# Folding two gain vectors into weight rows, and moving elementwise work off GpSimd, in a one-core decoder layer

## The chip, the cores and the metric

One core of a Trainium2 chip runs the whole program. The metric is device microseconds of one execution, the median over several runs. Engines are named as in the profile: PE is TensorE's matrix multiply (PEld its weight load), DVE is VectorE, ACT is ScalarE, POOL is GpSimd, SP is SyncE, whose queue issues nearly all transfers.

## The reference, cut to what matters

```python
h = rms_norm(x, g_mix)
z = h @ w_in                       # u, gb, gc, q, k, v
y_conv = gb * short_conv(gc * u, conv_w)
y_attn = dilated_mixture(q, k, v)  # q, k normed per head
mix = concat(rms_norm(y_conv, g_conv_out), rms_norm(y_attn, g_attn_out))
x = x + mix @ w_out
h = rms_norm(x, g_ffn)
x = x + (silu(h @ w_gate) * (h @ w_up)) @ w_down
# rms_norm(x, g) = x * rsqrt(mean(x*x) + 1e-6) * g ; SEQ 2048, D 1024, D_FF 2816, float32
```

A gain `g` that multiplies the columns of a normalised activation can as well multiply the rows of the weight that follows: `(n * g) @ W = n @ (diag(g) W)`. That identity is what the change uses, for `g_attn_out` with the lower half of the rows of `w_out`, and for `g_ffn` with the rows of `w_gate` and `w_up`.

## The kernel before, in words

Every float32 operand of a matrix product is held as two float16 parts, high and low, and each product is three passes on PE (high by high, high by low, low by high). Weights are first scaled by a power of two found from their largest absolute value (`vmax`, then `pow2`), then split: ACT writes the high part, DVE the low part as scaled input minus high part.

The stages, in the order of the profile's time:

- Up to about 245 us: the norm of `x`, the first projection with the gated convolution (`conv_steps`), and, in between, the splitting of later weights into DRAM. `spill_pair` does this for `w_out`, two column blocks of 256 at a time: L169 on ACT and L170 on DVE, each over 128 x 2048 elements.
- Up to about 856 us: attention, head pair by head pair (`attn_steps`), with the next pair's projections and the tail of the convolution woven in.
- About 856 to 1065 us, called the output stage here: `out_b`, a loop over p = 0 to 7, each pass with two row tiles of 128 (rows p and p + 8). `prep(p)` loads the attention output, squares it on ACT (L777), multiplies it by the row `g_attn_out` on POOL (L778), scales and splits it (L784 on ACT, L785 on DVE), and transposes it by transfers on SP's queue. `tiles(p)` runs the lower half of the output projection (`out_half`), adds each PSUM bank to the residual on DVE (L803, evacuation), squares the sum on ACT (L808), makes the norm's factor on DVE in a few tiny instructions (`rnorm`, L61 to L66), multiplies by factor and `g_ffn` on DVE (L812), forms four Strassen-Winograd sums on POOL (L816 to L819), and splits seven blocks into `hl` (ACT L825; L826 on DVE, the first of the four on POOL), which SP stores to `d_h` (L827). `out_a(p + 1)` runs the upper half of the projection for a later pass: split of its input (L728 on ACT, L729 on DVE), evacuation (L741 on DVE; L743 on ACT, then L744 on POOL). For p = 3 and 5 the first two calls of `left` are made here.
- From about 1040 to 1860 us: the gate and up products in the seven-product Winograd form, 11 rounds f. `left` prepares each round's weights, once for gate and once for up: load of 128 x 2048 elements into `raw`, `vmax` (L88) and `pow2` on DVE, four sums on POOL (L852 to L855), seven splits (L868 on ACT, L869 on DVE). `down` does the same for `w_down` and stores to DRAM (L908 to L914).
- To the end: the down product (L1069).

The queue of each engine is in order. Their order comes from a planner that simulates the program when it is built; `issue_after(x)` holds the instructions made inside it behind `x` on the engine of `x`. The `left` calls of p = 3 and 5 stand behind `self.dve`, `self.act` and `self.sp`.

Buffers that matter: `raw` (pool `wq`) has two, `t` of the Winograd sums one, `hl` one, the split weights `w` fifteen.

Of the kernel before, what the change touches and what calls it, by code (L numbers as in the profile page):

```python
# [29 lines left out]
class Builder:  # L30
# [22 lines left out]
    def rnorm(self, pool, ss, n, d, tag):  # L53


        nc = self.nc
        e = nc.vector
        y = pool.tile([P, n], F32, name=f"{tag}_y")
        t = pool.tile([P, n], F32, name=f"{tag}_t")
        v = pool.tile([P, n], F32, name=f"{tag}_v")  # L60
        nc.scalar.activation(y, ss, AF.Sqrt, scale=1.0 / d, bias=self.eps)  # L61
        e.tensor_scalar(v, ss, 1.0 / d, EPS, op0=ALU.mult, op1=ALU.add)
        e.reciprocal(y, y)
        e.scalar_tensor_tensor(t, y, -0.5, y, op0=ALU.mult, op1=ALU.mult)
# [91 lines left out]
    def spill_pair(self, cols, ux, dst, un):  # L156

        nc = self.nc
        raws = []
        for ap in cols:  # L160
            raw = self.wraw.tile([P, KC, 256], F32, name="wraw")
            nc.sync.dma_start(raw, ap.rearrange("(c p) n -> p c n", p=P))
            raws.append(raw)
        s, u = self.pow2(self.wsm, self.vmax(*(r.rearrange("p k c -> p (k c)") for r in raws)), "w", 14, 14)
        nc.vector.tensor_tensor(un, u, ux, op=ALU.mult)
        for i, raw in enumerate(raws):
            wh = self.wsp.tile([P, KC, 256], F16, name="wh")
            wl = self.wsp.tile([P, KC, 256], F16, name="wl")
            nc.scalar.activation(wh, raw, AF.Copy, scale=s)  # L169
            nc.vector.scalar_tensor_tensor(wl, raw, s, wh, op0=ALU.mult, op1=ALU.subtract)  # L170
            nc.sync.dma_start(dst[:, 0, :, 256 * i:256 * (i + 1)], wh)
            nc.sync.dma_start(dst[:, 1, :, 256 * i:256 * (i + 1)], wl)
# [21 lines left out]
    def run(self):  # L194
        tc, nc, A = self.tc, self.nc, self.A
        with ExitStack() as ctx:
# [16 lines left out]
            self.eps = cp.tile([P, 1], F32, name="eps")  # L213
# [16 lines left out]
    def setup(self):  # L230

        nc, A, cp = self.nc, self.A, self.cp
        make_identity(nc, self.ident32)
        nc.vector.memset(self.ones, 1.0)
        nc.vector.memset(self.eps, EPS)
# [396 lines left out]
    def attention_pairs(self):  # L632
# [28 lines left out]
        self.g_at_row = self.rows.tile([P, 512], F32, name="g_row3")  # L661
        nc.scalar.dma_start(self.g_at_row, A["g_attn_out"][0].partition_broadcast(P))
        nc.vector.tensor_scalar_mul(self.g_at_row, self.g_at_row, self.g_out[2])
# [84 lines left out]
    def out_b(self):  # L748
        tc, nc, A = self.tc, self.nc, self.A
        with ExitStack() as c:  # L750
            e = c.enter_context
            op = self.op = e(tc.tile_pool(name="op", bufs=1))
            g_at = self.g_at_row
            g_ffn = op.tile([P, D], F32, name="g_row2")
            nc.sync.dma_start(g_ffn, A["g_ffn"][0].partition_broadcast(P))
            self.g_ffn = self.row_scale(g_ffn, "gffn", 7)
            nc.vector.tensor_scalar_mul(g_ffn, g_ffn, self.g_ffn[1])
# [3 lines left out]
            def prep(p):  # L761
# [20 lines left out]
                r = self.rnorm(op, ss, 2, 512, "opr")  # L782
# [7 lines left out]
            def tiles(p, mt):  # L790
# [6 lines left out]
                for j in range(2):  # L797
# [23 lines left out]
                for src, q, n, e_ in ((xs[0].rearrange("p (a b) -> p a b", a=2), 0, 2, nc.gpsimd),  # L821
# [4 lines left out]
                    e_.tensor_tensor(o[:, :, 1], src, o[:, :, 0], op=ALU.subtract)  # L826
# [39 lines left out]
    def wsplit(self, x, s):  # L866
        w = self.fw.tile([P, 2, 4, P], F16, name="w")
        self.nc.scalar.activation(w[:, 0], x, AF.Copy, scale=s)  # L868
        self.nc.vector.scalar_tensor_tensor(w[:, 1], x, s, w[:, 0], op0=ALU.mult, op1=ALU.subtract)  # L869
        return w  # L870

    def left(self, w, f):
# [14 lines left out]
        for n in self.ORDER:  # L887
            W[n] = self.wsplit(src[n], s)
# [258 lines left out]
```

## Time and profile before

| what | value |
|---|---|
| median of 3 runs | 2265.3 us (2264.29 to 2267.96) |
| the profiled execution | 2265.61 us, its span 2263.8 us |
| mean granted TensorE clock | 0.973 |
| PE busy | 2134.7 us (94%) |
| DVE busy | 1538.1 us (68%) |
| ACT busy | 937.2 us (41%) |
| POOL busy | 787.9 us (35%) |
| SP's queue, share of 16 transfer engines | 55.9% |

The span runs from the first to the last instruction; what lies around it is the difference to the execution's time, 1.8 us. Busy shares are means over stages with different limits, so they say where to look and not what a change is worth.

### The profile page before, as it was taken

The page shows a single profiled execution, that of the slowest core. Times are in us where ns is not written, and L with a number is a line of the kernel's source. Part 1 is how long each engine was busy: PE and PEld are TensorE (multiplying, and loading weights), DVE is VectorE, ACT ScalarE, POOL GpSimd, SP SyncE. Part 2 cuts the span into 40 slices and gives each one's busy share as a digit, 9 for nine tenths or more (in the row PEclk, how much of TensorE's full clock was granted, in tenths as well). Part 3 has the DMA queues.
Part 4 walks back from the last instruction along what each step waited for, and adds up shares of the span by engine and source line. Part 5 has one row for each costly group of instructions (what it writes and reads, how often), then busy time and mean ns, then how long its engine had stood idle before and what let it go on. Part 6 is the DMA issues. An engine that isn't in the chain of part 4 may idle for free.

```text
span 2263.8 us, 32997 instructions
## 1 busy us (share of the span) xinstructions
PE 2134.7 (94%) x11816; PEld 1070.1 (47%) x11816; DVE 1538.1 (68%) x3265; ACT 937.2 (41%) x2112; POOL 787.9 (35%) x591
## 2 busy tenths in 40 slices
PE   4898999999999979788999999999999999999999
PEld 2344566666565544333444444444444444444444
DVE  6776457888777678796677676676767565555554
ACT  5422236666566655443333233233322343333341
POOL 3010243445444116554122122122222225555463
PEclk9999999999799989999999999999999999999999
DMA  9776356889789987669933322333223455152342
GB/s 242 163 227 224 95 125 126 185 153 168 170 154 183 215 207 222 217 186 257 222 117 107 98 89 89 103 112 99 88 98 105 144 171 203 56 186 60 118 144 93
DMA packets 568052, 340.68 MB, mean 150 GB/s; under 512 B 370896, under 2 KB 520400, under 8 KB 565456
## 3 DMA queue, kind: packets, MB, share of 16 engines
q1 hardware_dynamic: 564672, 337.72, 55.9%
q8 instruction: 92, 1.51, 0.3%
q10 hardware_dynamic: 3216, 0.86, 0.2%
q14 instruction: 72, 0.59, 0.1%
HBM read 162.34 MB, written 107.48 MB: 119 GB/s over the span
## 4 chain that ended last, share of the span: by engine, by line
PE 43%; DMA 4%; DVE 4%; SPq 3%; issue 1%; ACT 1%; POOL 1%; DVEq 0%; ACTq 0%; POOLq 0%
PE ps L951 25%; PE ps L1069 18%; SPq L191 2%; DMA d_wd<-w 1%; DVE w L869 1%; DMA wq<-in_w_up_dram 1%; DMA wq<-in_w_gate_dram 1%; ACT w L868 1%; DMA wq<-d_a 1%; DVE hl L826 0%; DVE vm_a L88 0%; DVE s L957 0%; DVE b L729 0%; SPq L877 0%; ACT wq L1047 0%
## 5 line engine op out<-in xcount | busy, mean ns | idle before, releaser
L951 PEld LDWEIGHTS <-w 128*128 128x128 f16 x3696 | 363.0, 98 | 459.4 <-issue 22.4
L951 PE MATMUL ps<-b,w 128*128 128x512 f16 x2112 | 469.5, 383 | 15.0 <-DVE s L957 6.7
L1069 PE MATMUL ps<-b,w 128*128 128x512 f16 x1848 | 399.3, 379 | 0.9 <-DVE s L1087 0.8
L951 PE MATMUL ps<-hb,w 128*128 128x512 f16 x1584 | 347.4, 379 | 0.9 <-DVE s L957 0.9
L1069 PEld LDWEIGHTS <-w 128*128 128x128 f16 x1848 | 180.8, 98 | 219.2 <-issue 1.4
L852 POOL TENSOR_TENSOR t<-wq 128x512 f32<-128x512 f32 (+1 forms) x46 | 59.1, 1285 | 501.8 <-issue 226.2
L581 ACT ACTIVATE sm<-sm,u 128x256 f32<-128x256 f32 (+1 forms) x384 | 173.9, 456 | 67.8 <-DVE u L576 65.9
L868 ACT ACTIVATE w<-t,w_s 128x512 f16<-128x512 f32 x132 | 94.8, 720 | 248.7 <-PE ps L951 120.4
L957 DVE TENSOR_TENSOR s<-ps,s 128x512 f32<-128x512 f32 x220 | 149.2, 684 | 41.3 <-PE ps L951 39.6
L576 DVE CUSTOM_DVE_ANT_0 sm<-s,mask,nkap 128x256 f32<-128x256 f32 (+1 forms) x384 | 144.1, 420 | 44.7 <-PE s L572 25.0
L183 PE MATMUL mm<-wq,b 128*128 128x384 f16 x512 | 171.7, 335 | 0.0
L184 PE MATMUL mm<-wq,b 128*128 128x384 f16 x512 | 171.4, 335 | 0.0
L185 PE MATMUL mm<-wq,b 128*128 128x384 f16 x512 | 171.1, 334 | 0.0
L1076 POOL TENSOR_TENSOR x<-x,s 128x512 f32<-128x512 f32 x72 | 103.2, 1434 | 186.0 <-DVE s L1087 131.3
L869 DVE SCALAR_TENSOR_TENSOR w<-t,w_s,w 128x512 f16<-128x512 f32 x132 | 98.8, 749 | 96.0 <-ACT w L868 95.9
L1077 DVE SCALAR_TENSOR_TENSOR x<-ps,a_u,x 128x512 f32<-128x512 f32 x96 | 72.0, 750 | 112.5 <-PE ps L1069 83.9
L868 ACT ACTIVATE w<-wq,w_s 128x512 f16<-128x512 f32 x99 | 71.3, 720 | 180.5 <-PE ps L951 66.9
L572 PE MATMUL s<-kb,qT 128*128 128x256 f16 (+1 forms) x384 | 131.1, 357 | 2.6 <-DMA kb<-klz 2.6
L571 PE MATMUL s<-ka,qT 128*128 128x256 f16 (+1 forms) x384 | 129.9, 355 | 2.9 <-DVE u L576 1.9
L593 DVE TENSOR_TENSOR eh<-sm,eh 128x512 f16<-128x512 f32 (+1 forms) x112 | 101.3, 907 | 40.8 <-ACT eh L592 40.3
L184 PEld LDWEIGHTS <-b 128*128 128x128 f16 x768 | 77.6, 101 | 90.6 <-issue 33.4
L183 PEld LDWEIGHTS <-b 128*128 128x128 f16 x768 | 77.6, 101 | 75.5 <-issue 6.9
(296 smaller groups left out, 3723.4 us busy)
## 6 DMA issues: line engine op xcount, KB each, us to landing
d_a<-a SPq DMA_DIRECT2D x88, 256.0 KB, 2.0
d_wd<-w SPq DMA_DIRECT2D x77, 256.0 KB, 2.0
wq<-d_a SPq DMA_DIRECT2D x64, 256.0 KB, 4.2
b<-d_wd SPq DMA_DIRECT2D x14, 1024.0 KB, 5.7
wraw<-in_w_in_dram SPq DMA_DIRECT2D x24, 512.0 KB, 7.3
v<-d_v SPq DMA_DIRECT2D x24, 512.0 KB, 4.6
d_h<-hl SPq DMA_DIRECT2D x24, 512.0 KB, 3.8
wq<-in_w_gate_dram SPq DMA_DIRECT2D x22, 512.0 KB, 5.2
```

The costliest lines, as they stand in the source:

```text
L183: self.pe = mm(ps, lhsT=lh(k), rhs=rh(k), start=k == ks[0], stop=False)
L184: mm(ps, lhsT=lh(k), rhs=rl(k), start=False, stop=False)
L185: mm(ps, lhsT=ll(k), rhs=rh(k), start=False, stop=k == ks[-1])
L571: nc.tensor.matmul(sp[:, at[u]], lhsT=q, rhs=cols(ka, u, pv), start=True, stop=False)
L572: nc.tensor.matmul(sp[:, at[u]], lhsT=q, rhs=cols(kl, u, pv), start=False, stop=True)
L576: nc.vector.tensor_tensor_reduce(sm[:, at[u]], sp[:, at[u]], self.mask[:, P - P * has_prev(u):256], accum_out=Ub[:, u, HD + 1:HD + 2], op0 ...
L581: nc.scalar.activation(sm[:, at[u]], sm[:, at[u]], AF.Exp, scale=-1.0, bias=Ub[:, u, HD + 1:HD + 2], accum_out=Ub[:, u, HD:HD + 1])
L868: self.nc.scalar.activation(w[:, 0], x, AF.Copy, scale=s)
L869: self.nc.vector.scalar_tensor_tensor(w[:, 1], x, s, w[:, 0], op0=ALU.mult, op1=ALU.subtract)
L951: nc.tensor.matmul(ps[self.BANK[n]], lhsT=w[:, x, k], rhs=b[:, y, k], start=first and k == 0 and q == 0, stop=k == 3 and q == 2, skip_grou ...
L957: nc.vector.tensor_tensor(t, x, y, op=ALU.add)
L1069: nc.tensor.matmul(ps[self.BANK[n]], lhsT=L[n][:, x, f], rhs=B[n][:, f, y], start=first and f == 0 and q == 0, stop=f == n_f - 1 and q == ...
```

## The change

`g_attn_out` no longer multiplies the attention output: `spill_pair` multiplies rows 512 to 1023 of `w_out` by it while it splits them, in five pieces for each column block (one of 128 x 1024, four of 128 x 256, each with its own factor column) instead of one. `g_ffn` no longer multiplies the normed activation: `left` multiplies the eight row blocks of each gate and up weight tile by it, in place, in eight ACT instructions of 128 x 256, ahead of the POOL sums; its seven splits are then without a factor. The two gain rows broadcast over partitions (L662 with L663, L755 with the lines behind it) go away; `g_ffn` is loaded as a 128 x 8 column tile on ACT's queue by `gains`. In the output stage L778 goes away, L812 moves from DVE to ACT, L816 to L819 and the first L826 move from POOL to DVE. `self.act` is now the scaling on ACT, `self.dve` the last L826. Powers of two shift between the factors (`SHIFTS`).

```diff
-    def rnorm(self, pool, ss, n, d, tag):
+    SHIFTS = (0, 8, 9)
+    def rnorm(self, pool, ss, n, d, tag, shift=0):
+        f = 4.0 ** -shift
...
-        nc.scalar.activation(y, ss, AF.Sqrt, scale=1.0 / d, bias=self.eps)
-        e.tensor_scalar(v, ss, 1.0 / d, EPS, op0=ALU.mult, op1=ALU.add)
+        b = self.SHIFTS.index(shift)
+        nc.scalar.activation(y, ss, AF.Sqrt, scale=f / d, bias=self.eps[:, b:b + 1])
+        e.tensor_scalar(v, ss, f / d, f * EPS, op0=ALU.mult, op1=ALU.add)
...
@@ spill_pair
-        s, u = self.pow2(self.wsm, self.vmax(...), "w", 14, 14)
+        s, u = self.pow2(self.wsm, self.vmax(...), "w", 13, 13)
         nc.vector.tensor_tensor(un, u, ux, op=ALU.mult)
+        sg = self.wsm.tile([P, 4], F32, name="w_sg")
+        nc.vector.tensor_scalar(sg, self.g_out[0][:, 4:8], s, 2.0 ** -9, op0=ALU.mult, op1=ALU.mult)
         for i, raw in enumerate(raws):
             wh = self.wsp.tile([P, KC, 256], F16, name="wh")
             wl = self.wsp.tile([P, KC, 256], F16, name="wl")
-            nc.scalar.activation(wh, raw, AF.Copy, scale=s)
-            nc.vector.scalar_tensor_tensor(wl, raw, s, wh, op0=ALU.mult, op1=ALU.subtract)
+            for k, f in [(slice(0, 4), s)] + [(4 + k, sg[:, k:k + 1]) for k in range(4)]:
+                nc.scalar.activation(wh[:, k], raw[:, k], AF.Copy, scale=f)
+                nc.vector.scalar_tensor_tensor(wl[:, k], raw[:, k], f, wh[:, k], op0=ALU.mult, op1=ALU.subtract)
...
@@ attention_pairs
-        self.g_at_row = self.rows.tile([P, 512], F32, name="g_row3")
-        nc.scalar.dma_start(self.g_at_row, A["g_attn_out"][0].partition_broadcast(P))
-        nc.vector.tensor_scalar_mul(self.g_at_row, self.g_at_row, self.g_out[2])
...
@@ out_b
-            g_ffn = op.tile([P, D], F32, name="g_row2")
-            nc.sync.dma_start(g_ffn, A["g_ffn"][0].partition_broadcast(P))
-            self.g_ffn = self.row_scale(g_ffn, "gffn", 7)
-            nc.vector.tensor_scalar_mul(g_ffn, g_ffn, self.g_ffn[1])
+            self.g_ffn = self.gains(self.cp, [A["g_ffn"][0]], "gffn", 0)
+            self.u_ffn = self.cp.tile([P, 1], F32, name="u_ffn")
+            nc.vector.tensor_scalar_mul(self.u_ffn, self.g_ffn[1], 2.0 ** -8)
...
@@ prep
                         nc.scalar.activation(hl[:, j, 0, cs], yb[:, j, cs], AF.Square, accum_out=ss[:, q, j:j + 1])
-                        nc.gpsimd.tensor_tensor(yb[:, j, cs], yb[:, j, cs], g_at[:, cs], op=ALU.mult)
...
@@ tiles
-                    self.act = nc.scalar.activation(xn, x1, AF.Square, accum_out=ss[:, j:j + 1])
+                    nc.scalar.activation(xn, x1, AF.Square, accum_out=ss[:, j:j + 1])
                     xs.append(xn)
-                r = self.rnorm(op, ss, 2, D, "n2")
+                r = self.rnorm(op, ss, 2, D, "n2", 8)
                 for j in range(2):
-                    self.dve = nc.vector.scalar_tensor_tensor(xs[j], self.x1[p][j], r[:, j:j + 1], g_ffn, op0=ALU.mult,
-                                                              op1=ALU.mult)
+                    self.act = nc.scalar.activation(xs[j], self.x1[p][j], AF.Copy, scale=r[:, j:j + 1])
...
-                g = nc.gpsimd
+                g = nc.vector
                 g.tensor_tensor(t[:, 1], b12, b11, op=ALU.subtract)
                 g.tensor_tensor(t[:, 3], b22, b12, op=ALU.subtract)
                 g.tensor_tensor(t[:, 2], b22, t[:, 1], op=ALU.subtract)
                 g.tensor_tensor(t[:, 0], b21, t[:, 2], op=ALU.subtract)
                 hl = op.tile([P, 7, 2, 512], F16, name="hl")
-                for src, q, n, e_ in ((xs[0].rearrange("p (a b) -> p a b", a=2), 0, 2, nc.gpsimd),
+                for src, q, n, e_ in ((xs[0].rearrange("p (a b) -> p a b", a=2), 0, 2, nc.vector),
...
-                    e_.tensor_tensor(o[:, :, 1], src, o[:, :, 0], op=ALU.subtract)
+                    self.dve = e_.tensor_tensor(o[:, :, 1], src, o[:, :, 0], op=ALU.subtract)
...
@@ wsplit, left
+        if s is None:
+            self.nc.scalar.copy(w[:, 0], x)
+            self.nc.vector.tensor_tensor(w[:, 1], x, w[:, 0], op=ALU.subtract)
...
-        nc.vector.tensor_tensor(un, u, self.g_ffn[0], op=ALU.mult)
+        nc.vector.tensor_tensor(un, u, self.u_ffn, op=ALU.mult)
+        sg = self.wsm.tile([P, KC], F32, name="w_sg")
+        nc.vector.tensor_scalar_mul(sg, self.g_ffn[0], s)
+        for k in range(KC):
+            nc.scalar.activation(raw[:, k], raw[:, k], AF.Copy, scale=sg[:, k:k + 1])
...
-            W[n] = self.wsplit(src[n], s)
+            W[n] = self.wsplit(src[n])
```

## Rows read from the trace of the kernel before

**Rows 1.** Windows: length, busy (x) of PE, PEld, DVE, ACT, POOL; clock, transfers.
```profile
856.00:1065.00 209.00, 176.32 (x756) 76.55 (x757) 175.94 (x255) 95.40 (x172) 124.03 (x89) 0.93 0.73 217
...
1160.00:1860.00 700.00, 696.41 (x3222) 315.22 (x3221) 476.38 (x828) 224.28 (x333) 160.33 (x126) 1.00 0.32 107
```

**Rows 2.** Waits of PE, 856 to 1065 us: total us, times, longest.
```profile
PE mm L183 <- DVE qT L803: 12.1, 5, 5.4
PE mm L183 <- DVE qT L741: 6.0, 1, 6.0
PE ps L951 <- DMA b<-d_h: 5.7, 2, 3.2
```

**Rows 3.** Groups on DVE, 856 to 1066 us: busy us, mean ns, idle before.
```profile
L729 DVE SCALAR_TENSOR_TENSOR b<-ya,ga,b 128x256 f16<-128x256 f32 x24 | 24.3, 1050 | 0.2 <-ACT b L728 0.2
L826 DVE TENSOR_TENSOR hl<-b,hl 128x1024 f16<-128x1024 f32 x16 | 23.8, 1487 | 10.1 <-ACT hl L825 10.1
L785 DVE SCALAR_TENSOR_TENSOR b<-yb,opr_y,b 128x512 f16<-128x512 f32 x14 | 15.4, 1132 | 1.9 <-ACT b L784 1.8
L826 DVE TENSOR_TENSOR hl<-ka,hl 128x512 f16<-128x512 f32 x8 | 12.7, 1590 | 2.6 <-ACT hl L825 2.6
L812 DVE SCALAR_TENSOR_TENSOR ka<-qT,n_y,g_row 128x1024 f32<-128x1024 f32 x10 | 12.4, 1281 | 0.1
```

**Rows 4.** Single lines: duration ns min/median/max, first and last start us.
```profile
L729 DVE SCALAR_TENSOR_TENSOR b<-ka,ga,b x8: 474/484/515, 828.7 to 847.1; 128x256 f16<-128x256 f32 x8
...
L826 DVE TENSOR_TENSOR hl<-b,hl x16: 1206/1226/2508, 891.1 to 1064.7; 128x1024 f16<-128x1024 f32 x16
...
L826 DVE TENSOR_TENSOR hl<-ka,hl x8: 679/1641/2541, 884.1 to 1057.6; 128x512 f16<-128x512 f32 x8
...
L785 DVE SCALAR_TENSOR_TENSOR b<-wq,opr_y,b x2: 742/743/744, 851.5 to 852.3; 128x512 f16<-128x512 f32 x2
```

**Rows 5.** Timeline of POOL (first) and DVE, 990 to 997 us: start, duration.
```profile
990.38 1.73 POOL L816 TENSOR_TENSOR b<-ka 128x512 f32<-128x512 f32 x1
...
994.88 1.44 POOL L744 TENSOR_TENSOR qT<-qT,xt 128x512 f32<-128x512 f32 x1
...
990.91 5.69 DVE L729 SCALAR_TENSOR_TENSOR b<-ya,ga,b 128x256 f16<-128x256 f32 x4
996.52 0.74 DVE L803 SCALAR_TENSOR_TENSOR qT<-mm,uo,qT 128x512 f32<-128x512 f32 x1
```

**Rows 6.** Groups on POOL, 856 to 1066 us.
```profile
L826 POOL TENSOR_TENSOR hl<-ka,hl 128x1024 f16<-128x1024 f32 x8 | 18.8, 2350 | 8.1 <-ACT hl L825 8.1
L778 POOL TENSOR_TENSOR yb<-yb,g_row 128x512 f32<-128x512 f32 x12 | 16.8, 1409 | 28.0 <-ACT b L777 24.3 <-issue 3.7
L819 POOL TENSOR_TENSOR b<-ka,b 128x512 f32<-128x512 f32 x8 | 12.6, 1580 | 0.1
...
L816 POOL TENSOR_TENSOR b<-ka 128x512 f32<-128x512 f32 x8 | 11.1, 1393 | 16.3 <-DVE ka L812 15.1 <-DVE opr_v L62 1.2
```

**Rows 7.** Timeline of DVE and ACT where the output stage begins.
```profile
850.41 1.22 DVE L121 TENSOR_REDUCE gffn_mx<-g_row 128x1 f32<-128x1024 f32 x1 [2.09 <-DMA g_row<-in_g_ffn_dram]
851.54 0.74 DVE L785 SCALAR_TENSOR_TENSOR b<-wq,opr_y,b 128x512 f16<-128x512 f32 x1
...
848.35 1.33 ACT L784 ACTIVATE b<-wq,opr_y 128x512 f16<-128x512 f32 x2 [0.82 <-DVE opr_y L66]
```

**Rows 8.** Timeline of ACT and PE where the output stage ends.
```profile
1063.62 1.04 ACT L825 CAST hl<-b 128x1024 f16<-128x1024 f32 x1 [3.69 <-POOL b L819]
...
1065.20 1.01 PE L951 MATMUL ps<-b,w 128*128 128x512 f16 x2 [2.69 <-ACT s L995]
```

**Rows 9.** Line L170 on DVE, as in rows 4.
```profile
L170 DVE SCALAR_TENSOR_TENSOR wl<-wraw,w_s,wh x4: 2351/2352/2352, 208.8 to 239.1; 128x2048 f16<-128x2048 f32 x4
```

**Rows 10.** L728 on ACT as in rows 4; POOL's L852, 1160 to 1860 us.
```profile
L728 ACT ACTIVATE b<-ka,ga x8: 492/495/512, 827.7 to 844.3; 128x256 f16<-128x256 f32 x8
...
L852 POOL TENSOR_TENSOR t<-wq 128x512 f32<-128x512 f32 x21 | 27.1, 1288 | 435.1 <-issue 226.2 <-DVE w L869 182.2 <-DVE w L1057 26.7
```

More of the change, by code (lines that the diff above doesn't have):

```diff
@@ L163, in spill_pair @@
             raws.append(raw)
-        s, u = self.pow2(self.wsm, self.vmax(*(r.rearrange("p k c -> p (k c)") for r in raws)), "w", 14, 14)
+        s, u = self.pow2(self.wsm, self.vmax(*(r.rearrange("p k c -> p (k c)") for r in raws)), "w", 13, 13)
         nc.vector.tensor_tensor(un, u, ux, op=ALU.mult)
+        sg = self.wsm.tile([P, 4], F32, name="w_sg")
+        nc.vector.tensor_scalar(sg, self.g_out[0][:, 4:8], s, 2.0 ** -9, op0=ALU.mult, op1=ALU.mult)
         for i, raw in enumerate(raws):
@@ L212, in run @@
             self.ones = cp.tile([P, 1], F32, name="ones")
-            self.eps = cp.tile([P, 1], F32, name="eps")
+            self.eps = cp.tile([P, 3], F32, name="eps")
             self.wsm = ctx.enter_context(tc.tile_pool(name="wsm", bufs=3))
@@ L234, in setup @@
         nc.vector.memset(self.ones, 1.0)
-        nc.vector.memset(self.eps, EPS)
+        for i, b in enumerate(self.SHIFTS):
+            nc.vector.memset(self.eps[:, i:i + 1], 4.0 ** -b * EPS)
         nc.scalar.square(self.ones, self.ones)
@@ L752, in out_b @@
             op = self.op = e(tc.tile_pool(name="op", bufs=1))
-            g_at = self.g_at_row
-            g_ffn = op.tile([P, D], F32, name="g_row2")
-            nc.sync.dma_start(g_ffn, A["g_ffn"][0].partition_broadcast(P))
-            self.g_ffn = self.row_scale(g_ffn, "gffn", 7)
-            nc.vector.tensor_scalar_mul(g_ffn, g_ffn, self.g_ffn[1])
+            self.g_ffn = self.gains(self.cp, [A["g_ffn"][0]], "gffn", 0)
+            self.u_ffn = self.cp.tile([P, 1], F32, name="u_ffn")
+            nc.vector.tensor_scalar_mul(self.u_ffn, self.g_ffn[1], 2.0 ** -8)
             mb = self.big.tile([P, 2, 2, 4, 2, P], F16, name="b5")
@@ L781, in prep @@
                 ss = ss[:, 0]
-                r = self.rnorm(op, ss, 2, 512, "opr")
+                r = self.rnorm(op, ss, 2, 512, "opr", 9)
                 for j in range(2):
@@ L864, with wsplit @@
     NP = NF // 2
-    def wsplit(self, x, s):
+    def wsplit(self, x, s=None):
         w = self.fw.tile([P, 2, 4, P], F16, name="w")
-        self.nc.scalar.activation(w[:, 0], x, AF.Copy, scale=s)
-        self.nc.vector.scalar_tensor_tensor(w[:, 1], x, s, w[:, 0], op0=ALU.mult, op1=ALU.subtract)
+        if s is None:
+            self.nc.scalar.copy(w[:, 0], x)
+            self.nc.vector.tensor_tensor(w[:, 1], x, w[:, 0], op=ALU.subtract)
+        else:
+            self.nc.scalar.activation(w[:, 0], x, AF.Copy, scale=s)
+            self.nc.vector.scalar_tensor_tensor(w[:, 1], x, s, w[:, 0], op0=ALU.mult, op1=ALU.subtract)
         return w
@@ L878, in left @@
                               w[:, (f + self.NP * h) * P:(f + self.NP * h + 1) * P].rearrange("(c p) n -> p c n", p=P))
-        s, u = self.pow2(self.wsm, self.vmax(raw.rearrange("p a b -> p (a b)")), "w", 12, 12)
+        s, u = self.pow2(self.wsm, self.vmax(raw.rearrange("p a b -> p (a b)")), "w", 11, 11)
         un = self.wsm.tile([P, 1], F32, name="w_un")
-        nc.vector.tensor_tensor(un, u, self.g_ffn[0], op=ALU.mult)
+        nc.vector.tensor_tensor(un, u, self.u_ffn, op=ALU.mult)
[3 more added lines that the diff above has]
+            nc.scalar.activation(raw[:, k], raw[:, k], AF.Copy, scale=sg[:, k:k + 1])
         a11, a12, a21, a22 = (raw[:, 4 * k:4 * k + 4, h * P:(h + 1) * P] for h in range(2) for k in range(2))
```

## The prediction

> **What bounds the kernel now.** I read the windows by stage first. From 1160 to 1860 us PE is busy 696.4 of 700 us at clock 1.00, so nothing that the other engines give up there can shorten it much; 3222 matmuls in 700 us also give the full-speed price of one, 0.217 us. The output stage, 856 to 1065 us, is different: 756 matmuls at that price are 164 us, the stage takes 209, so 45 us are lost, and the granted clock is 0.93 [rows 1]. DVE is busy 175.9 us of it (84%), POOL 124.0, ACT 95.4. This is the stage that the change rewrites, and no engine is full in it.
>
> The waits of PE come next: who ends PE's idle time? Two lines on DVE, the evacuations L803 and L741, end 12.1 and 6.0 us; 5.7 us more end with the transposes that load `d_h` for the next stage [rows 2]. So DVE is late for PE, although it isn't always busy. Why it is late shows in the groups of DVE against the same lines undisturbed. L729 takes 1050 ns in the mean; the eight of it that ran before the stage took 484. The first L826 form (128x512) takes 1590 ns against a least of 679, the second (128x1024) 1487 against 1206, L785 1132 against 743 [rows 3, 4]. The timeline shows one case: POOL runs L816, then others up to L744, without a pause; meanwhile four L729 on DVE take 5.69 us, and L803, for which PE waits, comes only behind them at 996.52 [rows 5]. A VectorE instruction with two SBUF inputs thus lengthens by about one GpSimd instruction when it meets one. The evacuations, which read PSUM, stay at 0.74.
>
> **The change part by part.** The sum is made against the profiled execution's 2265.6 us (span 2263.8 and 1.8 around it), 0.3 above the median.
>
> *POOL's work in the output stage.* The lengthening of the four groups is 24 x (1.050 - 0.484) = 13.6, 16 x (1.487 - 1.206) = 4.5, 14 x (1.132 - 0.743) = 5.4 and 8 x (1.590 - 0.679) = 7.3, together 30.8 us of DVE time. The change takes from POOL the L826 form (18.8 us), L778 (16.8) and four lines L816 to L819, of 11.1 to 12.6 us each, some 47 [rows 6]: 83 of 124 us, or 67%. L744 and the weight sums remain. If lengthening goes with POOL's busy time, 0.67 x 30.8 = 20.6 us return.
>
> The Trainium skill, "SBUF — State Buffer", section "SBUF: two separate sides", says that VectorE with two SBUF inputs and GpSimd hold a shared pair of ports exclusively, each for a whole instruction. The trace agrees (rows 5). By that rule the sums that move to DVE can be blocked as well, so less returns than goes with POOL's busy time, and the forecast would be some 7 us later, at 2257.
>
> *What DVE takes over.* For each of eight p: four sums of 128x512 and one L826 of 128x1024 come, two L812 go. The trace has no such sum on DVE; the nearest row is the 679 ns of the 128x512 L826. That is 8 x (4 x 0.679 + 1.206 - 2 x 1.281) = +10.9 us [rows 3, 4]. Net for DVE: -20.6 + 10.9, about -10 us. ACT takes the two 1024-wide scalings, 1.04 us each going by a cast of that width [rows 8]: +17 us on 95.4 busy of 209 [rows 1], which I cost at nothing; if ACT were late for the casts, DVE would wait there as it does now (10.1 us) [rows 3].
>
> *What reaches the end.* PE waits 18.1 us for the two evacuations [rows 2], so I let all 10 us pass: -10. Bounds: 0, if DVE's new work sits exactly ahead of the evacuations, and -18 if both waits vanish. The clock gives something back too: 0.93 over 209 us is 14.6 us of lost speed [rows 1], and the matmuls behind a gap are the slow ones; a third of the idle gone is worth -3 (0 to -10).
>
> *Where the stage begins.* DVE waits 2.09 us for the broadcast row of `g_ffn`, then reduces it for 1.22 us, and only then, at 851.54, takes the first L785, whose scaled input ACT began at 848.35 and had after half of its 1.33 us, at 849.1 [rows 7]. The row goes away; the 128x8 gains live in a pool that exists from the start, so their load can be early. -2 us. If the load is planned at the same place, with its some fifteen tiny DVE instructions, nothing is won: 0.
>
> *Where it ends.* The last 1024-wide cast waits 3.69 us for L819 on POOL; ACT's PSUM copy stands behind it, and PE waits 2.69 us for that copy [rows 8]. On DVE the sum takes about half of POOL's time, and it starts at once: -2.7 (0 at the other end).
>
> *The split of `w_out`.* One L170 of 2.35 us becomes 1.206 + 4 x 0.484 = 3.14 [rows 4, 9]: +0.8, four times, 3.2 us of DVE, and much the same on ACT. It lies ahead of attention, between conv steps. 0 to +3.2; I take +1.
>
> *`left`.* Eight scalings of 0.495 us add 4.0 us to ACT for each of 22 calls [rows 10], some 72 us of them from 1160 to 1860 us, where ACT is busy 224 of 700 [rows 1]. They also add a wait: POOL's sums L852 to L855 can't start before ACT has scaled, and ACT can't before DVE has the factor. Behind the waiting L852 stand L744 and the sums of `down`; behind the scalings on ACT stand PSUM copies and Silu, for which PE waits. The cover is large: L852 idles 435 us over 21 calls, 20.7 each, and what ends it is the one buffer `t` (DVE's last split) or POOL's own order, never the load [rows 10]. I take +1 for the rounds whose weights are late anyway; with the cover gone it would be 4 us in each of ten rounds, +40. The first two calls also stand behind the last L826 of their tile now and no longer behind L812, some 7 us of DVE work later; their weights are first used after the stage's last transposes, so nothing. Dropping the row of `g_attn_out` removes a transfer and a small DVE pass: nothing.
>
> Sum: -10 - 3 - 2 - 2.7 + 1 + 1 = -15.7, so 2265.6 - 15.7 = 2249.9; I say 2250.
>
> **The rivals.**
>
> *More than that (0.14).* The tiny instructions of the norm, on whose factor ACT waits, are lengthened too and aren't in my 30.8. If PE's whole 18 us and most of the clock's loss return, -18 - 10 - 4.7 = -33: 2233. For it: no engine is full once POOL is light. Against: DVE would still be busy some 166 us of 175.
>
> *The rest of POOL keeps blocking (0.10).* By the code 26 of POOL's 512-wide sums stay in the stage (fourteen L744, twelve of the weights). If each still costs DVE, the moved sums among its victims, half of a POOL sum of 1.4 us [rows 6], that is 18 of the 30.8 us, and only 13 return: 2257. For it: L744 falls among DVE's L729 in rows 5. Against: less of DVE's queue is behind a given POOL instruction when POOL runs rarely.
>
> *The gain is swallowed (0.16).* The transposes of `d_h` come from one queue, and PE already waits 5.7 us for them [rows 2]. If they start no earlier, because the stores of the last pass or the weights of the first round bound them, the stage ends where it did, and only the entry and little else is left: about 2262. Against: the buffers into which they load come free with the projection's last matmuls, and these move.
>
> *DVE becomes the bound, slower (0.12).* The sums stand in DVE's queue ahead of L803. If the lengthening returns only below 10.9 us, the point from which this decides, the moved work is a net cost; with 4 us returned (L729 meets L744 anyway) it is +7, and PE waits that much longer, with +2 for spill and weights: 2275. For it: DVE is at 84%, and POOL was the idler engine. Against: rows 3 and 4 show twice that return.
>
> *The scalings of `left` land on the path, slower (0.08).* If they are placed in ACT's queue ahead of a PSUM copy, 4 us in each of ten rounds, less the stage's gain: 2265.6 + 40 - 16 = 2290. Against: ACT is at a third.
>
> **How the numbers follow.** The forecast as worked out has 0.40. Its own range: the return at either end moves it by 8, the clock by 3 to 7, the entry and end by 4.7, the rest by 3; these don't all fall together, so 2240 to 2259. About 0.2% (4.5 us) is what a measurement of this kernel can tell from no change. Faster by more than that: the forecast's 0.40, the larger gain's 0.14, most of the blocking case (0.08) and a quarter of the swallowed one (0.04), 0.66. Within it: the rest of those two, 0.14, and an edge of the slower ones, 0.01. Slower: 0.19. The range leaves out the two slower cases: 2233 to 2267, 0.8.
>
> **What would show it.** In the changed profile L729 should be near 500 ns, DVE's L826 near their least values, POOL below 45 us in the stage, and PE's waits for L803 and L741 below half. The first `out_half` of `out_b` should start about 2 us sooner relative to attention's end. From 1160 us on, PE's idle should stay near 4 us. I'm wrong if DVE's busy time in the stage doesn't fall, if PE's waits move from L803 to the new sums' place in the queue, or if a wait of POOL or PE for the eight scalings appears in the rounds.

## The result, and the profile after

The changed kernel takes 2251.13 us (median of 6 runs, 2249.72 to 2253.54) against 2265.46 for the kernel before (6 runs): ratio 0.9935, 95% interval 0.9924 to 0.9946. In the profiled executions the span falls from 2263.8 to 2251.7 us. The forecast of 2250 is met, but its terms are not: the stage gave almost twice what was forecast, and about half of that was lost again at two places where the forecast saw a gain or nothing. That the sum came out near is luck.

To see this, cut the span at three events: the first `out_half` of `out_b` (its first product into a `ps` bank), the first product with an `hb` tile (the transposes of the second half have arrived), and the first product of the down projection.

| us | before | after | difference |
|---|---|---|---|
| start of `out_b`'s first `out_half` | 856.4 | 859.8 | +3.4 |
| from there to the first `hb` product | 233.7 | 206.0 | -27.7 |
| from there to the first product of `down`'s projection | 769.8 | 781.9 | +12.1 |
| from there to the end of the span | 403.9 | 404.0 | +0.1 |

**The stage.** Windows of both kernels, first the one before (columns as in rows 1), then the one after with its long stretch of products:

```profile
856.00:1090.00 234.00, 201.11 (x864) 87.47 (x865) 187.63 (x271) 100.17 (x178) 124.03 (x89) 0.93 0.77 220
```
```profile
860.00:1066.00 206.00, 191.50 (x865) 85.27 (x864) 153.19 (x276) 117.93 (x203) 48.29 (x37) 0.97 0.85 238
...
1160.00:1848.00 688.00, 686.16 (x3179) 310.83 (x3178) 460.63 (x837) 262.81 (x468) 155.96 (x126) 1.00 0.33 109
```

The same matmuls (864 and 865 in the windows) in 28 us less; POOL falls from 124 to 48 us, DVE from 188 to 153, and ACT bears 18 more. In the long stretch PE idles 1.8 us of 688, before 3.6 of 700 [rows 1]. PE's waits in the stage after, whole, answer to [rows 2]:

```profile
PE ps L962 <- DMA b<-d_h: 8.9, 2, 8.3
PE mm L191 <- DVE kb L807: 3.7, 1, 3.7
PE mm L191 <- DVE qT L807: 1.9, 2, 1.3
```

Before, two more lines of the same view belong to the evacuations, which the forecast did not count:

```profile
PE mm L183 <- DVE kb L803: 3.4, 1, 3.4
...
PE mm L183 <- DVE kb L741: 2.6, 2, 1.7
```

So the evacuations' waits fall from 24.1 us (12.1 + 6.0 + 3.4 + 2.6) to 5.6. The groups on DVE after, 859 to 1048 us (L735 is L729 of before, L829 is L826, L789 is L785; L820 is one of the four sums that moved):

```profile
L829 DVE TENSOR_TENSOR hl<-b,hl 128x1024 f16<-128x1024 f32 x16 | 20.6, 1306 | 0.0
L735 DVE SCALAR_TENSOR_TENSOR b<-ya,ga,b 128x256 f16<-128x256 f32 x22 | 11.8, 569 | 0.0
L789 DVE SCALAR_TENSOR_TENSOR b<-yb,opr_y,b 128x512 f16<-128x512 f32 x14 | 10.2, 753 | 1.5 <-ACT b L788 1.5
...
L829 DVE TENSOR_TENSOR hl<-ka,hl 128x512 f16<-128x512 f32 x8 | 7.6, 953 | 0.0
...
L820 DVE TENSOR_TENSOR b<-ka 128x512 f32<-128x512 f32 x8 | 6.6, 820 | 0.0
...
L69 DVE TENSOR_TENSOR opr_t<-opr_t,opr_v 128x2 f32<-128x2 f32 x6 | 0.9, 158 | 0.1
```

Against [rows 3], 1050 ns has become 569, 1132 753, 1590 953 and 1487 1306. The norm's instructions, two numbers per partition, were lengthened too; two groups of before, 860 to 1045 us:

```profile
L65 DVE TENSOR_TENSOR opr_t<-opr_t,opr_v 128x2 f32<-128x2 f32 x6 | 5.1, 857 | 0.1
L66 DVE SCALAR_TENSOR_TENSOR opr_y<-opr_t,opr_y 128x2 f32<-128x2 f32 x6 | 4.4, 737 | 0.0
```

Both take 158 to 159 ns after. ACT's scaling L784 waited 20.3 us for the last of them in the stage before.

**The entry.** DVE's timeline after, where the factor `ga` (L353) for the first L735 is made:

```profile
819.04 0.17 DVE L92 TENSOR_REDUCE vm_a<-yamax 128x1 f32<-128x16 f32 x1
819.12 0.15 DVE L92 TENSOR_REDUCE vm_a<-gffn_g 128x1 f32<-128x8 f32 x1
...
829.29 0.15 DVE L79 TENSOR_SCALAR gffn_e<-gffn_m 128x1 int32<-128x1 int32 x1
...
829.69 0.23 DVE L353 TENSOR_SCALAR ga<-gout_g,ya_s 128x4 f32<-128x4 f32 x1
...
830.99 0.48 DVE L735 SCALAR_TENSOR_TENSOR b<-ka,ga,b 128x256 f16<-128x256 f32 x1
```

The reduction and powers of `g_ffn` run step by step between those of `yamax`: from `vm_a` to `ga` it is 10.65 us, and was 8.61 (818.82 to 827.43). PE's waits of 805 to 862 us, first before (where L734 is L728), then after:

```profile
PE mm L183 <- ACT b L728: 6.7, 2, 5.8
...
PE ps L183 <- DMA b<-b: 3.4, 1, 3.4
```
```profile
PE mm L191 <- ACT b L734: 11.8, 2, 7.0
```

Part of the 5.1 us more is hidden, since the wait of 3.4 us for the first transposes of the attention output is gone. The first `out_half` follows attention's last product (L600, after L609; 842.6 us, after 845.3) by 13.8 us before and by 14.5 after.

**The boundary of the first two rounds.** SP's timeline, before and after:

```profile
1022.87 1.23 SPq L877 DMA_DIRECT2D wq<-in_w_gate_dram  x2
...
1079.07 27.91 SPq L191 DMA_TRANSPOSE hb<-d_h  x6
...
1111.88 1.58 SPq L877 DMA_DIRECT2D wq<-in_w_up_dram  x2
```
```profile
1057.55 27.70 SPq L199 DMA_TRANSPOSE hb<-d_h  x6
...
1091.53 1.58 SPq L884 DMA_DIRECT2D wq<-in_w_gate_dram  x2
1093.21 3.08 SPq L884 DMA_DIRECT2D wq<-in_w_up_dram  x2
```

Before, round 1's gate weights were asked for ahead of most of the transposes and only its up weights behind them. Now both stand behind all of them. DVE's reduction of them waits for the DMA with PSUM sums (L968) queued behind it, and PE waits for those; DVE's timeline after, then PE's:

```profile
1098.25 2.29 DVE L92 TENSOR_REDUCE vm_a<-wq 128x1 f32<-128x2048 f32 x1 [1.82 <-DMA wq<-in_w_gate_dram]
...
1101.79 2.29 DVE L92 TENSOR_REDUCE vm_a<-wq 128x1 f32<-128x2048 f32 x1 [0.54 <-DMA wq<-in_w_up_dram]
...
1104.09 0.68 DVE L968 TENSOR_TENSOR s<-ps,s 128x512 f32<-128x512 f32 x1
```
```profile
1104.82 7.67 PE L962 MATMUL ps<-hb,w 128*128 128x512 f16 x24 [5.10 <-DVE s L968]
1116.78 1.03 PE L962 MATMUL ps<-b,w 128*128 128x512 f16 x2 [4.28 <-ACT w L872]
```

In the 100 us from 1066 PE does 369 matmuls at clock 0.91; in the 100 us from 1090 of the kernel before, 436 at 0.98. The 67 missing ones, at 0.217 us, are 14.5 us.

### The profile page after: what moved, and what is told of

Its sections match the earlier page's. It is cut to its first block, busy times and chain, and to the rows that moved or that the text cites. A ratio compares the mean times of both kernels' runs of the same rounds, so it can differ in the third digit from the quotient of the medians.

```text
span 2251.7 us, 33200 instructions
## 1 busy us (share of the span) xinstructions
PE 2132.3 (95%) x11816; PEld 1069.2 (47%) x11816; DVE 1506.8 (67%) x3337; ACT 1009.8 (45%) x2320; POOL 698.7 (31%) x533
## 4 chain that ended last, share of the span: by engine, by line
PE 73%; DVE 9%; DMA 8%; ACT 4%; issue 3%; SPq 2%; POOL 0%; DVEq 0%; ACTq 0%; POOLq 0%
PE ps L962 31%; PE ps L1080 18%; PE mm L191 5%; PE mm L192 5%; PE mm L193 5%; PE s L580 3%; PE s L581 3%; DMA et<-eh 3%; PE av L609 2%; DMA wraw<-in_w_in_dram 2%; DVE hl L829 1%; SPq L199 1%; DVE vm_a L92 1%; PE pt L596 1%; DMA b<-b 1%
## 5 line engine op out<-in xcount | busy, mean ns | idle before, releaser
L968 DVE TENSOR_TENSOR s<-ps,s 128x512 f32<-128x512 f32 x220 | 150.2, 684 | 43.7 <-PE ps L962 43.1
L602 DVE TENSOR_TENSOR eh<-sm,eh 128x512 f16<-128x512 f32 (+1 forms) x112 | 106.3, 951 | 42.9 <-ACT eh L601 42.3
L191 PEld LDWEIGHTS <-b 128*128 128x128 f16 x768 | 77.3, 101 | 76.6 <-ACT b L734 12.3
L192 PEld LDWEIGHTS <-b 128*128 128x128 f16 x768 | 77.4, 101 | 71.2 <-issue 12.9
L191 PE MATMUL cvx<-b,wq 128*128 128x512 f16 (+1 forms) x200 | 78.3, 392 | 32.4 <-ACT ka L271 26.3
L193 PEld LDWEIGHTS <-b 128*128 128x128 f16 x768 | 77.0, 100 | 65.4 <-issue 5.4
L872 ACT CAST w<-t 128x512 f16<-128x512 f32 x88 | 53.6, 615 | 105.5 <-PE ps L962 85.9
```

The source lines that it names most:

```text
L191: self.pe = mm(ps, lhsT=lh(k), rhs=rh(k), start=k == ks[0], stop=False)
L192: mm(ps, lhsT=lh(k), rhs=rl(k), start=False, stop=False)
L193: mm(ps, lhsT=ll(k), rhs=rh(k), start=False, stop=k == ks[-1])
L602: nc.vector.tensor_tensor(eh[:, w:2 * w], sm[:, 0:w], eh[:, 0:w], op=ALU.subtract)
L968: nc.vector.tensor_tensor(t, x, y, op=ALU.add)
```

## The experiments

Each ratio is to the kernel before, on the same chip (2261.4 to 2262.0 us there, 5 rounds). The stretches are those of the table above, from one execution each; the start scatters by several us between kernels whose instructions ahead of it differ little (in move_alone attention itself ended 6 us sooner), so verdicts on the start rest on the waits and chains there.

| run | ratio | 95% | start | stage | to `down` |
|---|---|---|---|---|---|
| left_early | 0.9880 | 0.9863 to 0.9897 | 858.9 | 206.9 | 766.4 |
| no_scale | 0.9910 | 0.9892 to 0.9928 | 858.3 | 206.3 | 773.2 |
| pool_back | 1.0032 | 1.0019 to 1.0045 | 858.3 | 229.8 | 775.6 |
| move_alone | 0.9928 | 0.9911 to 0.9946 | 851.0 | 217.1 | 771.5 |
| gains_early | 0.9856 | 0.9841 to 0.9872 | 852.2 | 203.9 | 769.3 |
| attn_fold_dve | 0.9915 | 0.9902 to 0.9929 | 856.1 | 212.2 | 768.9 |
| attn_fold_alone | 0.9937 | 0.9924 to 0.9950 | 850.9 | 221.7 | 766.2 |
| idle_pool_work | 0.9992 | 0.9981 to 1.0002 | 860.9 | 226.9 | 768.2 |
| gains_no_scale | 0.9905 | 0.9891 to 0.9919 | 857.0 | 207.4 | 772.4 |
| gains_pool_back | 0.9958 | 0.9941 to 0.9975 | 853.1 | 221.7 | 768.7 |
| evac_dve | 0.9856 | 0.9838 to 0.9873 | 852.0 | 202.4 | 767.1 |
| scale_twice | 0.9876 | 0.9853 to 0.9899 | 856.3 | 205.7 | 768.8 |

**left_early** and **no_scale**: was the 12 us a matter of place, or of the scalings?

```diff
-                if p in (3, 5):
+                if p in (2, 4):
```

> The changed kernel with the first two calls of left made one pass earlier (p = 2 and 4 for 3 and 5); nothing else differs. The load of the second round's gate weights then stands ahead of most of the transposes of d_h on SP's queue, behind all of them in the changed kernel. Theory A (the output stage gained some 23 us, and 12 of them were given back where the second round begins, since that load came late): PE's waits at that boundary, 12.2 us in the changed kernel, fall to 2 to 5, and the time to about 2243. Theory B (the give-back is the scaling work itself, on ACT and in the chain to POOL's sums, wherever the load stands): the waits stay above 9 us, 2249 to 2252.

> The changed kernel with left as it was before: the eight scalings on ACT are left out and the splits carry the factor again, so g_ffn is left out of the computation. It shows what the folding of g_ffn costs in the weights. Theory A: only the first boundary pays, since the load of the second round's gate weights comes ahead of most transposes here too: 2241 to 2244, the same as with left called earlier. Theory B (scalings cost in every round): clearly below the run with left called earlier, by 0.4 us or more per round, 2236 to 2240 against 2244 or more. My prediction's term for left was +1 us.

no_scale takes the scalings out of `left`, so `g_ffn` is left out of the computation, and uses the split of before:

```diff
-        for k in range(KC):
-            nc.scalar.activation(raw[:, k], raw[:, k], AF.Copy, scale=sg[:, k:k + 1])
...
-            W[n] = self.wsplit(src[n])
+            W[n] = self.wsplit(src[n], s)
```

left_early measured 0.9880, 12 us under the changed kernel's ratio on a base of 2261. Its gate load of round 1 stands at 1001.62, again ahead of most of the transposes, and PE has these waits in the 100 us from 1066:

```profile
PE ps L962 <- DVE s L968: 3.6, 4, 1.7
PE ps L962 <- DVE w L873: 1.1, 2, 0.8
```

It does 437 matmuls there. One pair of numbers in the code, with all scalings in place, returns the whole loss: the place of the calls, and with it of the load, is the cause. no_scale's gate load, at 1008.12, is ahead of most transposes too, and half of the loss goes.

Why the load stands where it does shows in the buffer that it takes, which round 0's up weights leave. The last split on DVE that reads it (L869; L873 or L876 in the others) ends at 1022.84 us before, at 1001.56 in left_early and at 1008.06 in no_scale, and the load follows within 0.1 us. In the changed kernel it ends at 1023.5, as late as before in a stage that is 28 us shorter, and the program has the load behind the transposes. no_scale has the same markers as the changed kernel, so a later marker alone is not the cause: the scalings hold the buffer as well, since POOL's sums of these weights wait for them (first the changed kernel, then no_scale, where the same pair of sums runs 38 us sooner):

```profile
1007.04 1.27 POOL L856 TENSOR_TENSOR t<-wq 128x512 f32<-128x512 f32 x1 [12.27 <-ACT wq L892]
```
```profile
969.11 1.53 POOL L855 TENSOR_TENSOR t<-wq 128x512 f32<-128x512 f32 x1 [19.90 <-DVE hl L829]
```

Taking the scalings away or making the calls sooner each brings the load forward. Why no_scale keeps the other half of the loss stays open.

**scale_twice** and **gains_no_scale**: what do the scalings cost where they stand well?

```diff
             nc.scalar.activation(raw[:, k], raw[:, k], AF.Copy, scale=sg[:, k:k + 1])
+            if f > 0:
+                nc.scalar.copy(raw[:, k], raw[:, k])
```

> gains_early (0.986) with each of the eight scalings of `left` followed by a second ACT copy of the same tile in place, for the weights of rounds 1 to 10: 160 ACT instructions of 0.49 us more, 79 us, and GpSimd's sums start 4 us later in each of the twenty calls. The output stage has the same instructions in the same order. Theory: the scalings are hidden in the rounds, so doubling them costs nothing there (0.984 to 0.987), but for some 4 us if the first rounds' boundary is still tight (0.988). Rival (the forecast's slower case): they lie on the path of the rounds; 4 us for each of ten rounds is 40 us, 1.003, and 4 us for each call twice that.

> gains_early (ratio 0.986) with `left` as in the kernel before: no scalings, so `g_ffn` is left out of the computation. It prices the scalings where they stand well. Theory: with the loads ahead of the transposes ACT's eight scalings of 0.49 us and the wait of GpSimd's sums for them are hidden in all rounds, the forecast's +1 was right for the scalings themselves, and the ratio stays at 0.984 to 0.987. Rival: they still cost at the boundary of the first rounds even there, and without them the ratio is 0.982 or less.

The added copies are in the groups of ACT from 1050 to 1840 us, and PE's waits from 1065 to 1830 are 6.7 us in all (gains_early, from 1060: 7.7):

```profile
L893 ACT ACTIVATE wq<-wq,w_sg 128x256 f32<-128x256 f32 x152 | 62.7, 494 | 32.4 <-DVE w_sg L891 32.4
L895 ACT COPY wq<-wq 128x256 f32<-128x256 f32 x152 | 51.1, 398 | 0.0
```

51 us more of ACT and a later start of GpSimd's sums leave the stretch at 768.8 against 769.3: the scalings are hidden in the rounds. (The interval of the whole time overlaps gains_early's; the start, 856.3 us against 852.2, accounts for the 4 us between the medians.) gains_no_scale was missed by both theories: without the scalings the kernel is slower than with them. Its weights' sums no longer wait for ACT, and a fourth reduction of weights falls into the stage; L739 (L735 of the changed kernel) is at 647 ns against 528, and PE waits 10.4 us for L808 against 3.0. Which of these makes the difference, and how much of it is the start at 857.0, stays open; no price of the scalings can be read from this pair.

**pool_back**, **move_alone**, **attn_fold_alone**, **attn_fold_dve**: the parts by themselves.

```diff
-                g = nc.vector
+                g = nc.gpsimd
...
-                for src, q, n, e_ in ((xs[0].rearrange("p (a b) -> p a b", a=2), 0, 2, nc.vector),
+                for src, q, n, e_ in ((xs[0].rearrange("p (a b) -> p a b", a=2), 0, 2, nc.gpsimd),
```

That is pool_back, the folds without the move; move_alone is the same two lines the other way in the kernel before. attn_fold_dve is the changed kernel with `g_ffn` handled as before, and attn_fold_alone adds pool_back's two lines to it:

```diff
-            self.g_ffn = self.gains(self.cp, [A["g_ffn"][0]], "gffn", 0)
...
+            self.g_ffn = self.row_scale(g_ffn, "gffn", 7)
...
-                    self.act = nc.scalar.activation(xs[j], self.x1[p][j], AF.Copy, scale=r[:, j:j + 1])
+                    self.dve = nc.vector.scalar_tensor_tensor(xs[j], self.x1[p][j], r[:, j:j + 1], g_ffn, op0=ALU.mult,
+                                                              op1=ALU.mult)
...
-            W[n] = self.wsplit(src[n])
+            W[n] = self.wsplit(src[n], s)
```

> The changed kernel with the four sums and the first split of hl back on GpSimd. Theory of the prediction (GpSimd's instructions lengthen DVE's two-input ones, and that makes the evacuations late): L735 returns to about 800 ns or more from 561, PE's waits for the evacuations to 10 us or more, and the time to 2258 to 2264. Rival (the gain came from the dropped multiplication by g_attn_out and from the scaling's move to ACT): 2249 to 2254.

> The kernel before with only the four sums and the first split of hl given to DVE: no folding, so DVE keeps the scaling by g_ffn, GpSimd keeps the product with g_attn_out, and left has no scalings. Theory of the prediction: 66 of GpSimd's 124 us in the stage go, some 16 of 30.8 us of lengthening return, DVE takes on about 31 us (four sums 2.7 and a split 1.2 in each of eight passes), so DVE is busier by about 15: 2262 to 2272, no gain. Theory C (the latency of GpSimd's sums, not DVE's time, was the loss): the stage is shorter by 10 or more, about 2252.

> The kernel before with the fold of `g_attn_out` alone: GpSimd's sixteen multiplications L778 are gone (16.8 of its 124 us in the stage), the sums stay on GpSimd, `g_ffn` is as before. Theory of lengthening: VectorE's time returns with GpSimd's share, 16.8/124 of 30.8 us, 4 us, ratio 0.998. Theory of GpSimd's queue (its results are late, and L778 stands ahead of them): the sums start up to 1.4 us sooner for each of eight p, 8 to 11 us, ratio 0.995 to 0.996. Nothing at all, or slower, would say that the fold pays only together with the sums' move.

> The changed kernel without the fold of `g_ffn`: its row is loaded, reduced and multiplied on VectorE as in the kernel before, `left` has no scalings, and the gate load has its place of before; the fold of `g_attn_out` and the sums on VectorE stay. Theory: the fold of `g_ffn` gives the stage about 10 us (16 L812 of 1.28 us leave VectorE) and costs about as much at the boundary of the first two rounds, so without it the stage takes 175 to 180 us, from the first `hb` product to the first product of `down` it is 766 to 772, and the ratio is 0.990 to 0.993. Rival 1: the fold of `g_ffn` is what made the stage fast, and move_alone's gain came from its earlier entry; then the ratio is 0.995 or more. Rival 2: the fold of `g_ffn` costs more than it gives, and without it the ratio is 0.986.

The move alone is worth 16 us, as much as the whole change, where the theory of the prediction expected no gain. L729 is at 736 ns there (1050 before), so some lengthening went; but with its new work VectorE was busier than before, 191.4 us in the stage against 187.3, and the stage is 16.6 us shorter all the same:

```profile
851.00:1068.10 217.10, 195.41 (x864) 85.95 (x865) 191.39 (x307) 99.42 (x176) 61.17 (x49) 0.96 0.82 232
```

So VectorE's busy time alone doesn't explain the stage. That results come sooner when they don't wait for GpSimd (latency) is the likely rest; no run takes it alone, and its size is not shown. The fold of `g_attn_out` alone is worth 14 us, the fold and the move together 19. pool_back, slower than expected, is taken up with gains_pool_back. Adding the fold of `g_ffn` as it was made turns 0.9915 into 0.9935, though it shortens the stage by 6 us. attn_fold_alone gave more than either theory said. L735 is as slow there as before (1077 ns), but other groups are shorter (L831, the L826 of before, 1359 and 1114 ns for 1487 and 1590; L790, before L785, 1017 for 1132; the norm's small instructions 19.6 us in all for 25.8), and VectorE's busy time in the stage falls from 187.3 to 174.4 us. PE's waits for the evacuations fell from 24.1 to 16.6 us. The multiplications L778 also stand no longer in GpSimd's queue ahead of the sums. Lengthening, the queue and the sooner start (attention ended 6.7 us sooner in this execution, the fastest of its five) are not separated in this run.

**idle_pool_work** and **gains_pool_back**: lengthening or latency?

```diff
+                with tc.issue_after(self.act.ins):
+                    for _ in range(2):
+                        for k in range(2):
+                            nc.gpsimd.tensor_tensor(z[:, k], z[:, k], z[:, 1 - k], op=ALU.subtract)
+                    nc.gpsimd.tensor_tensor(z[:, 0:2], z[:, 0:2], z[:, 0:2], op=ALU.subtract)
...
+            z = op.tile([P, 2, 512], F32, name="z")
+            nc.gpsimd.memset(z, 0.0)
```

This is added to left_early.

> left_early (0.988) with useless work for GpSimd: for each p four sums of 128x512 and one of 128x1024 on a tile of its own, which nothing else reads, at the place of the sums that were taken from it. VectorE's own work is unchanged, and no result is late but what stands behind them in GpSimd's queue. Theory of lengthening (GpSimd's instructions lengthen VectorE's two-input ones): some 65 us of GpSimd's work return, L735 goes from 528 ns to about 900, VectorE gets 15 to 25 us longer in the stage, and the ratio is 0.995 to 1.000. Theory of latency (the gain came from sums that no longer wait in GpSimd's queue and run in half the time): L735 may lengthen, but the time stays within 5 us of left_early, ratio 0.988 to 0.990.

> gains_early (0.986) with the four sums and the first `hl` difference of each p on GpSimd again: both folds alone, with their loads and gains well placed. Theory of lengthening (as idle_pool_work showed, 24 us): 20 to 24 us come back, ratio 0.995 to 0.997, and the folds with GpSimd's sums are worth about what the fold of `g_attn_out` alone was, 0.994. Rival: pool_back's loss (1.003) came from the place of the loads and gains, and the move is worth only some 12 us when they stand well: 0.991.

Work that nobody reads costs 25 us (0.9880 to 0.9992), 20 of them in the stage. VectorE has the same instructions as in left_early, and from 860 to 1045 us it waits for no result of GpSimd. (ACT does once, 2.8 us: a small copy that it needs stands behind the idle sums.) From the start of `out_b`'s first `out_half` to the first `hb` product VectorE is busy 28 us longer; left_early first:

```profile
858.90:1065.80 206.90, 191.02 (x866) 84.83 (x865) 157.97 (x291) 122.73 (x213) 41.20 (x37) 0.98 0.88 248
```
```profile
860.90:1087.80 226.90, 196.43 (x864) 85.93 (x865) 185.75 (x292) 123.19 (x213) 96.99 (x72) 0.95 0.80 224
```

Some of its groups, with left_early's means of 537, 1280 and 404 ns for them, are now

```profile
L735 DVE SCALAR_TENSOR_TENSOR b<-ya,ga,b 128x256 f16<-128x256 f32 x23 | 15.0, 679 | 0.0
L834 DVE TENSOR_TENSOR hl<-ka,hl 128x1024 f16<-128x1024 f32 x7 | 11.4, 1633 | 0.6 <-ACT hl L833 0.6
...
L68 DVE SCALAR_TENSOR_TENSOR n_t<-n_y 128x2 f32<-128x2 f32 x7 | 6.0, 862 | 0.2
```

and PE's longest wait of the stage is back:

```profile
PE mm L191 <- DVE qT L807: 14.8, 5, 6.8
```

It was 2.8 us in left_early. The time follows the theory of lengthening; the expected 900 ns of L735 did not come, and the norm's small instructions (up to 862 ns) and the sums took more of it. gains_pool_back puts the useful work back on GpSimd and loses 23 us, as expected; by the difference to pool_back's 1.0032, some 17 us there were the place of loads and gains. VectorE's busy time in the stage is only 3 us above gains_early's there (163.1 to 160.3), with 40 instructions fewer, and the stage is 18 us longer: here too busy time alone doesn't explain it.

**gains_early**: `self.g_ffn`, `self.u_ffn` and their chain, in left_early, made in attention's first group and not in `out_b`:

```diff
             for n, _ in enumerate(a):
+                if g == 0 and n == 10:
+                    self.g_ffn = self.gains(self.cp, [A["g_ffn"][0]], "gffn", 0)
...
```

> The changed kernel with the two early calls of `left` moved one tile forward (as in left_early, ratio 0.988), and in addition the 128x8 gains of `g_ffn` loaded, reduced and scaled during the last conv steps and not at the head of `out_b`. Theory E: the entry came 3.4 us later and not 2 earlier because some fifteen tiny VectorE instructions for `g_ffn` stand, from 819 to 831 us, between the steps of the chain that gives the factor of the first L735 (828.66 before, 830.99 after). Then the first L735 comes about 2.3 us sooner, PE's wait for ACT b L734 at 805 to 862 falls from 11.8 us to some 7, the first `out_half` of `out_b` starts 3 to 5 us sooner, and the ratio to the kernel before is 0.986. Rival: that entry is set by attention's last steps whatever VectorE has to do, and the time stays at left_early's 0.988.

The ratio is the expected 0.986; its interval just overlaps left_early's. The chain has its old length again, 8.66 us, and PE's wait its old size:

```profile
815.87 0.16 DVE L92 TENSOR_REDUCE vm_a<-yamax 128x1 f32<-128x16 f32 x1
...
824.53 0.22 DVE L353 TENSOR_SCALAR ga<-gout_g,ya_s 128x4 f32<-128x4 f32 x1
```
```profile
PE mm L191 <- ACT b L738: 5.9, 2, 5.0
```

The other runs bear this out: PE waits 11.8 to 12.3 us for this line in the five that have the `g_ffn` chain at the head of `out_b` (the changed kernel, left_early, no_scale, pool_back, idle_pool_work) and 5.8 to 6.7 in the nine others.

**evac_dve**: GpSimd's part of the evacuations in `out_a`, from p = 2 on, given to VectorE, in gains_early.

```diff
-                if m < 1:
+                if m < 1 or p > 1:
                     nc.vector.scalar_tensor_tensor(xc, ps, u, xc, op0=ALU.mult, op1=ALU.add)
```

> gains_early (0.986) with the second evacuation of each `out_half` of `out_a` from p = 2 on done in one VectorE instruction from PSUM (0.74 us) in place of an ACT copy and GpSimd's L750. GpSimd then has only the two weights' sums and small copies in the stage. Theory: VectorE gets 12 of 0.74, 9 us, and of the lengthening that is left (L735 at 528 against 484, the 1024-wide differences at 1.28 against 1.21, one sum at 0.99 against 0.82, the norm's small instructions) some 6 to 8 us return, so the time stays within 3 us: 0.985 to 0.988. Rival 1: VectorE is the bound now and all 9 us show, 0.990. Rival 2: what is left of GpSimd still costs more than its replacement, 0.983.

POOL falls to 24 us from 860 to 1030 (40 in gains_early), DVE stays at 141 (143) in spite of nine us more work, and the ratio is the same 0.9856. With gains_early it is the best version: 1.44% under the kernel before, where the change as made has 0.65%.

## Why the prediction was right in sum and wrong in its terms

- *The return of VectorE's time, -10, and the clock, -3.* That GpSimd's work lengthens VectorE's instructions and so costs PE time is shown (idle_pool_work); that it is the whole gain of the stage is not (move_alone). The sizes were too small. The forecast let 20.6 of 30.8 us return; by the four groups it was 25 (24 x 0.489, 16 x 0.181, 14 x 0.379 and 8 x 0.637 us, with 561 ns for all 24 of L735), and 10 more by the norm's small instructions (70 of them, 25.8 to 15.8 us), which the larger rival had named. The moved work came out as priced: four sums of 0.68 to 0.82 us and one difference of 1.27, less two L812, are 8 x (2.94 + 1.27) - 22 = +12, against +10.9. That leaves -23 on DVE by these groups; its whole busy time in the stage fell from 187.6 to 153.2 us. The second error was the cap: PE's waits for the evacuations were 24.1 us and not 18.1, since only the two longest lines were read; 18.5 of them went. The third was the clock: 0.93 over 234 us is 16.4 us of lost speed and 0.97 over 206 is 6.2, so 10.2 came back, the far bound; PE's busy time for the same products fell by 9.6 (201.1 to 191.5).
- *The end, -2.7.* Right: the wait of [rows 8] is gone.
- *The transposes.* The rival of the swallowed gain showed in part: the wait for `d_h` rose from 5.7 to 8.9 us, +3.2. The stage by these rows: -18.5 - 10.2 - 2.7 + 3.2 = -28.2; measured -27.7.
- *The entry, -2.* Wrong, +3.4, and +0.7 counted from attention's last product. The wait for the broadcast row of [rows 7] did go. The forecast looked at when the new load could be issued and costed the small instructions behind it only at that place; the program put them 20 to 30 us earlier, among the steps of the chain that the first L735 needs. gains_early took that back.
- *`left`, +1.* The scalings themselves are hidden in the later rounds, as was argued (scale_twice), and the slower rival, 4 us in each round, fell. The sentence that failed is that the early calls' place costs nothing: it asked when these weights are used, and not when their buffer comes free. `wq` has two buffers; with the scalings ahead of POOL's sums the one for the next gate load came free no sooner than before, the load stood behind 28 us and more of transposes in SP's queue, and 12 us were lost one round later (left_early, no_scale).
- *The spill of `w_out`, +1.* Not tried by itself. Its DVE instructions came about as priced (1.28 + 4 x 0.48 = 3.2 us for 2.35), and attention's first product with `et` stands at 326.3 us, 328.0 before, so no loss shows.
- *The rivals.* "More than that" was near for the stage (-30.7 named without its entry, -28 measured). "The rest of POOL keeps blocking" and "DVE becomes the bound" did not happen. The Trainium skill, "SBUF — State Buffer", section "SBUF: two separate sides", says that a VectorE instruction with two SBUF inputs and a GpSimd instruction that reads SBUF shut each other out for a whole instruction. By that rule the moved sums can be blocked as well; the traces agree (L822, one of the sums, took 683 ns in the changed kernel, 1035 in left_early and 1274 in idle_pool_work). The 7 us that the forecast gave to it were not lost: the four sums took 2.94 us in the mean of a pass, 2.72 as priced.
- *The signs.* L735 (561 ns), the evacuations' waits (24.1 to 5.6 us) and the rounds (1.8 us of idle) came as named. The L826 of before did not come near its least values (1306 and 953 ns for 1206 and 679), POOL kept 48 us and not below 45, and the entry came no sooner.

## What to carry to other kernels

Where VectorE works beside GpSimd, look at what GpSimd does before trimming VectorE: here even useless GpSimd work cost 25 us, and the tiny instructions of a norm were lengthened as the wide ones were. When work is put between a load and the last reader of its buffer, follow that buffer to the next load in the DMA queue and to what stands ahead of that load. A handful of tiny instructions is free only off the chains, so ask for them long before anything waits, and sum all lines of a wait, not the longest two.

## What the hardware showed beyond that

GpSimd's instructions are lengthened at times too. Eight of L750 took 2067 ns in the mean in the changed kernel, and 1456 before (as L744); left_early, with the same work on both engines, has 1423, and the least of any is 1.26 us. So it isn't the amount of VectorE's work that decides; which instructions meet may be the reason, but no run tests it:

```profile
L750 POOL TENSOR_TENSOR qT<-qT,xt 128x512 f32<-128x512 f32 x8 | 16.5, 2067 | 43.3 <-ACT xt L749 35.2 <-DMA d_h<-hl 8.0
```

Instructions of two elements per partition took up to 0.86 us in the mean of a group, in place of 0.16. The evacuations from PSUM took 0.74 us in every version.
